# Hybrid streaming encoder on one core: the merge's first weights staged in the merge's own pool, the recurrence's state update in the PSUM bank of its outputs, four buffers for gate tiles

## The chip, the cores and the metric

The kernel runs on one core of one Trainium2 chip. Its time is the device time of one execution in microseconds (us); the time of a kernel is the median of its runs. The engines are named as in the profile: PE (TensorE, matmuls), PEld (its weight loads), DVE (VectorE), ACT (ScalarE), POOL (GpSimd) and SP (SyncE, which issues most DMAs). Every engine takes its instructions strictly in the order in which they stand in the program. SP does so too: a DMA that waits for a buffer holds up every DMA behind it.

## The reference, cut to what matters

One layer over 1024 prompt rows and 64 sample rows, model width 1024:

```
u = rms_norm(x)
proj = u @ w_in                      # four branches' inputs, and the gates
out_b = branch_b(proj)               # fox, diff, sb: attention; gdn: a recurrence
merged = sum_b sigmoid(gates_b) * (out_b @ w_branch[b])
x = x + merged @ w_out
x = x + swiglu(rms_norm(x))
y = rms_norm(x)

# gdn, per chunk of 64 rows:
v_new = u_i - kc_i @ S
o     = (q_i * exp(g_i)) @ S + a_i @ v_new
S     = S * exp(g_last) + (k_i * exp(g_last - g_i))^T @ v_new
```

The gates are a matmul of u with 4 x 1024 columns of `w_in`. They depend on nothing but u, so they can be computed at any time before the merge.

## The kernel before

The kernel is written as one long Python function; a scheduler then orders the instructions of each engine, by the priorities of the code and its own estimate of times. Precision is kept by splitting every operand into a high and a low float16 part, so that each product is three matmuls (`gemm_a`, lines 177 to 186).

The work goes in stages, and two of them matter here.

**The attention stages.** `attend_sb`, `attend_fox` and `attend_diff` run one after the other. In `attend_diff` (line 627) two pairs of heads go through nine tiles of 128 rows each, from the longest to the shortest. For one head of one tile PE computes scores (line 456, a mask at 458), DVE takes their maximum (646), ACT the exponential (655), DVE combines two softmaxes and splits the result, SP transposes it by DMA (`pt`, line 447), and PE multiplies by the values (lines 604 and 606). After each head `fill` (line 505) takes other work from two lists:

- `dense`: work that keeps PE busy. At this point it is `spill_gates` (line 1056). One call loads 256 columns of gate weights, in two DMAs of 512 KB to `w32` (line 149), splits them to `wh` (ACT) and `wl` (DVE), and computes six pieces of 128 gate rows, each of 24 matmuls to a bank `pgs`. ACT moves each piece to a tile `ths` in SBUF, and POOL's queue writes it to DRAM (line 1067).
- `side`: in `attend_diff` first the recurrence `gdn_seq` (line 896), one chunk of 64 rows per call, then `open_merge` (line 1128).

**The recurrence.** Each of 17 chunks computes `kc @ S` to `pks` (lines 1008 and 1009), `vn` on DVE, its split `vh`, the state update `pds` (12 matmuls, line 1021), the output `pog` (20 matmuls, lines 1024 to 1028), and the new state on DVE (line 1029), which is split to `Sh` and `Sl` for the next chunk. `prepare` (line 954) makes the next tile's operands. All PSUM tiles of the recurrence come from `pgd`, two banks: `pog` holds one for a whole tile, with `pks` in its upper half, and `pds`, `py`, `pu`, `pk` take turns.

**The merge.** `open_merge` closes the recurrence's pool and opens the merge's pool `br` in its place, then calls `load_branch` for `sb` and for `fox`. `load_branch` (line 1109) brings the branch's output (`oT`) and its two blocks of weights (512 KB each, line 1123), which are staged in `w32` and split to `wbh` and `wbl`, tiles of `br`. The loop from line 1162 then takes the branches in the order sb, fox, diff, gdn. For each of 24 pieces per branch it loads the gate tile from DRAM (`thg`), ACT applies tanh (1174), PE computes six matmuls to `ptb`, DVE multiplies, and DVE or POOL adds to the accumulators `mg`. For sb the gate tiles rotate over four buffers, for the others over twelve. `drain(dense)` (line 1140) puts whatever is left of the gates ahead of the merge's main part.

The staging tile `w32` has three buffers for the whole kernel. Each is held from the DMA's issue until DVE has made the low part from it:

```
w32 = wp.tile([P, 4, BW], F32, tag="w32", name="wb32", bufs=3)
wv = w32.rearrange("p a b -> p (a b)")[:, :D]
sync.dma_start(wv, i["w_branch"][0][j, k * P:(k + 1) * P])
acopy(wbh[:, k], wv, WS)
stt(wbl[:, k], wv, WS, wbh[:, k], ALU.mult, ALU.subtract)
```

Of the kernel before, what the change touches and what calls it, by code (L numbers as in the profile page):

```python
# [11 lines left out]
F32 = mybir.dt.float32  # L12
# [5 lines left out]
P = 128  # L18
D = 1024
KD = D // P  # L20
SEQ, SMP, PAST = 1024, 64, 256
T = SEQ + SMP
NT = 9
NH = 4
BW = 256
# [28 lines left out]
def tile_hybrid_encoder(ctx, tc, i, o):  # L54
# [8 lines left out]
    def stt(out, in0, s, in1, op0, op1):  # L63
        return vec.scalar_tensor_tensor(out=out, in0=in0, scalar=s, in1=in1, op0=op0, op1=op1)  # L64

    def tt(out, in0, in1, op, eng=None):
        return (eng or vec).tensor_tensor(out=out, in0=in0, in1=in1, op=op)
# [6 lines left out]
    def bc(ap, shape):  # L74
        return ap.to_broadcast(shape)
# [6 lines left out]
    wp = ctx.enter_context(tc.tile_pool(name="w", bufs=2, reuse_waits="tile"))  # L82
# [12 lines left out]
    def pgd(name="pgd"):  # L95
        return pp.tile([P, 512], F32, tag="g", name=name, bufs=2)
# [120 lines left out]
    sp = sp_.enter_context(tc.tile_pool(name="sp", bufs=1, side="right", reuse_waits="tile"))  # L217
# [674 lines left out]
    def new_state(S32, Sh, Sl):  # L892
        acopy(Sh, S32, 16.0)
        stt(Sl, S32, 16.0, Sh, ALU.mult, ALU.subtract)

    def gdn_seq(g3):
        ttbd = []
        for q in range(2):
            a = g3.tile([P, 2, NH, P], F16, name=f"ttbd{q}")
# [4 lines left out]
        for q in range(2):  # L904
            a = g3.tile([P, NH, 64], F32, name=f"tt32{q}")
# [6 lines left out]
        for q in range(2):  # L912
            a = g3.tile([P, 2, NH, 64], F16, name=f"vh{q}")
# [3 lines left out]
        def fresh_state():  # L917
            return (g3.tile([P, NH, 64], F16, tag="Sh", name="Sh", bufs=2),
                    g3.tile([P, NH, 64], F16, tag="Sl", name="Sl", bufs=2))
# [74 lines left out]
        for k, t in enumerate(order):  # L994
            after = load(order[k + 1]) if k + 1 < len(order) else None
            _, n, nch, u0, kc, kd, aa, qe, zt = here
            z4g = zt.rearrange("p (h e) -> p h e", h=NH)
            S32 = S32s if t == 8 else S32p
            if t in (8, 0):
                Sh, Sl = fresh_state()  # L1000
                new_state(S32, Sh, Sl)
            po = pgd("pog")
            pks = po[:, 256:512]
            for c in range(nch):
                sl = slice(64 * c, 64 * c + 64)
                e4 = eg[:, c, t * NH:(t + 1) * NH]
                for h in range(NH):
                    pe.matmul(pks[sl, h * 64:h * 64 + 64], lhsT=kc[:, h, sl], rhs=Sh[:, h], start=True, stop=False)
                    pe.matmul(pks[sl, h * 64:h * 64 + 64], lhsT=kc[:, h, sl], rhs=Sl[:, h], start=False, stop=True)
                S1 = g3.tile([P, NH, 64], F32, tag="S1", name="S1", bufs=2)  # L1010
                tt(S1, S32, bc(e4[:, :, None], [P, NH, 64]), ALU.mult)
                vn = g3.tile([P, NH, 64], F32, tag="vn", name="vn", bufs=2)
                vh = vhs[c]
                stt(vn[sl].rearrange("p h e -> p (h e)"), pks[sl, 0:256], -(2.0 ** -5),
                    u0[sl].rearrange("p h e -> p (h e)"), ALU.mult, ALU.add)
                acopy(vh[sl, 0], vn[sl])
                tt(vh[sl, 1], vn[sl], vh[sl, 0], ALU.subtract)
                pds = pgd("pds")
                for h in range(NH):
                    for q, (a, b) in enumerate(((0, 0), (0, 1), (1, 0))):  # L1020
                        pe.matmul(pds[:, h * 64:h * 64 + 64], lhsT=kd[:, a, h], rhs=vh[:, b, h], start=(q == 0), stop=(q == 2))
                for h in range(NH):
                    dst = po[sl, h * 64:h * 64 + 64]
                    pe.matmul(dst, lhsT=qe[:, h, sl], rhs=Sh[:, h], start=True, stop=False)
                    pe.matmul(dst, lhsT=qe[:, h, sl], rhs=Sl[:, h], start=False, stop=False)
                    pe.matmul(dst, lhsT=aa[:, 0, h], rhs=vh[:, 0, h], start=False, stop=False)
                    pe.matmul(dst, lhsT=aa[:, 0, h], rhs=vh[:, 1, h], start=False, stop=False)
                    pe.matmul(dst, lhsT=aa[:, 1, h], rhs=vh[:, 0, h], start=False, stop=True)
                stt(S32.rearrange("p h e -> p (h e)"), pds[:, 0:256], 2.0 ** -9, S1.rearrange("p h e -> p (h e)"), ALU.mult, ALU.add)
                Sh, Sl = fresh_state()  # L1030
                if not (t == 8 or (t == 7 and c == 1)):
                    new_state(S32, Sh, Sl)
                if c == 0 and after is not None:
                    here = prepare(*after)
                yield 0.0
            if t == 8:
                gps.dma_start(o["s_gdn_state"][0, 0].rearrange("h d e -> d h e"), S32[0:64])
            if t == 7:
                gps.dma_start(o["p_gdn_state"][0, 0].rearrange("h d e -> d h e"), S32[0:64])
            sq = g3.tile([P, NH, 64], F32, tag="sqo", name="sqo", bufs=1)  # L1040
            pov = po[:n, 0:256].rearrange("p (h e) -> p h e", h=NH)
            act.activation(sq[:n], pov, AF.Square)
            ss = g3.tile([P, NH], F32, tag="sso", name="sso", bufs=2)
            vec.tensor_reduce(out=ss[:n], in_=sq[:n], op=ALU.add, axis=AX.X)
            ts(ss[:n], ss[:n], 2.0 ** -18 / 64, EPS, ALU.mult, ALU.add, eng=gps)
            tt(ss[:n], ss[:n], mhb[:n, 0:NH], ALU.pow, eng=gps)
            tt(z4g[:n], z4g[:n], bc(ss[:n, :, None], [n, NH, 64]), ALU.mult)
            tt(z4g[:n], z4g[:n], pov, ALU.mult)
            os_ = g3.tile([P, 2, BW], F16, tag="osg", name="osg", bufs=2)
            acopy(os_[:n, 0], zt[:n])  # L1050
            tt(os_[:n, 1], zt[:n], os_[:n, 0], ALU.subtract)
            gps.dma_start(od["gdn"][t * P:t * P + n], os_[:n].rearrange("p l c -> p (l c)"))
# [3 lines left out]
    def spill_gates(b, sp, d2):  # L1056
        j = bidx[b]
        wu = load_unit([(w_in, 0, OFF_GATE + j * D + d2 * BW, BW)], BW)
        for m in range(2):
            d = 2 * d2 + m  # L1060
            for off, n in PIECES:
                pg = pd("pgs")
                gemm_a(pg, wu, m * P, uh, ul, off, n, KD)
                th = sp.tile([P, 364], F32, tag="ths", name="ths", bufs=2)
                with tc.high_priority():
                    acopy(th[:, :n], pg[:, :n], 0.5 * IWS)
                gps.dma_start(gtd[b][d * P:(d + 1) * P, off:off + n], th[:, :n])
                yield 3.7
# [40 lines left out]
    def load_branch(b):  # L1109

        brp, j = brps[0], bidx[b]
        oT = brp.tile([P, 2, 2, T], F16, tag="oT", name="oT", bufs=2)
        if b in ("sb", "fox"):
            for pr in range(2):
                gps.dma_start(oT[:, :, pr], od[b][pr])
        else:
            sync.dma_start_transpose(out=oT.rearrange("p l r t -> p (l r) t"), in_=od[b])
        wbh = brp.tile([P, 2, D], F16, tag="wbh", name="wbh", bufs=2)
        wbl = brp.tile([P, 2, D], F16, tag="wbl", name="wbl", bufs=2)
        for k in range(2):  # L1120
            w32 = wp.tile([P, 4, BW], F32, tag="w32", name="wb32", bufs=3)
            wv = w32.rearrange("p a b -> p (a b)")[:, :D]
            sync.dma_start(wv, i["w_branch"][0][j, k * P:(k + 1) * P])
            acopy(wbh[:, k], wv, WS)
            stt(wbl[:, k], wv, WS, wbh[:, k], ALU.mult, ALU.subtract)
        branch[b] = oT, wbh, wbl

    def open_merge():
        gd_.close()
        brps.append(br_.enter_context(tc.tile_pool(name="br", bufs=1, side="right", reuse_waits="tile")))  # L1130
        load_branch("sb")
        yield 0.0
        load_branch("fox")
        yield 0.0

    side += [gdn_seq(g3), open_merge()]
# [2 lines left out]
    brp = brps[0]  # L1139
# [16 lines left out]
    gt_pool = gp_.enter_context(tc.tile_pool(name="gates", bufs=1, reuse_waits="tile"))  # L1156

    pbk = (psc, pgd, psc, pgd, psc)
    nb_ = [0]
    mg = [(brp if d < 3 else gt_pool).tile([P, T], F32, tag=f"mg{d}", name=f"mg{d}") for d in range(KD)]  # L1160
    order = ("sb", "fox", "diff", "gdn")
    for bi, b in enumerate(order):
        if b not in branch:
# [5 lines left out]
        for d, (off, n) in [(d, PIECES[p]) for p in (0, 2, 1) for d in range(KD)] if last else \  # L1169
                [(d, p) for d in range(KD) for p in PIECES]:  # L1170
            th = (brp if bi == 0 else gt_pool).tile([P, 364], F32, tag=("th0" if bi == 0 else "th"), name="thg",
                                                    bufs=(4 if bi == 0 else 12))
# [366 lines left out]
```

## Time and profile before

| | |
|---|---|
| median of 3 runs | 1920.94 us (1919.0 to 1921.34) |
| the profiled execution's own time | 1923.47 us |
| its span, first to last instruction | 1921.5 us |
| PE busy | 92% of the span |
| DVE busy | 65% |
| ACT busy | 45% |
| POOL busy | 16% |
| granted TensorE clock, mean | 0.954 |

The table's shares are averages over the whole program. The kernel is bound by different things in different stages, so the stretches between about 640 and 1145 us are looked at one by one below. Times within the profile count from the span's start. A busy PE is an engine that has matmuls in flight; how fast they go depends on the granted clock.

### The profile page before, as it was taken

How to read it: one execution, taken by the hardware profiler on the slowest of the kernel's cores; microseconds unless marked ns; L12 is line 12 of the kernel's file. 1: busy time of each engine (PE TensorE's matmuls, PEld its weight loads, DVE VectorE, ACT ScalarE, POOL GpSimd, SP SyncE). 2: the span in 40 equal slices, each digit the busy share in tenths (PEclk: the TensorE clock that was granted, in tenths of full speed). 3: DMA queues.
4: the chain of work that ended last, by engine and by line, in shares of the span. 5: the costliest groups of instructions: out<-in, count | busy, mean ns of one | idle time of the engine just before them, and what ended most of it. 6: DMA issues, size and time to landing. Idle time of an engine off the chain costs nothing.

```text
span 1921.5 us, 36810 instructions
## 1 busy us (share of the span) xinstructions
PE 1767.0 (92%) x14364; PEld 1252.4 (65%) x14364; DVE 1249.0 (65%) x2589; ACT 868.2 (45%) x1819; POOL 310.3 (16%) x478
## 2 busy tenths in 40 slices
PE   7999898989977998766799889999999999999998
PEld 5678774656755565444466558886857758677573
DVE  7559773877776667889411997766646546556365
ACT  6335654998654455556522463433413314233142
POOL 2113341111001222212211661000000000000002
PEclk9999999999989999566899999999999999999999
DMA  6267789887989855444733955621211212112112
GB/s 222 44 108 218 224 234 215 168 179 155 208 191 210 183 148 128 94 108 84 262 107 103 280 153 144 121 83 34 78 44 45 67 32 79 45 45 67 33 45 99
DMA packets 412766, 244.28 MB, mean 127 GB/s; under 512 B 266278, under 2 KB 390450, under 8 KB 412456
## 3 DMA queue, kind: packets, MB, share of 16 engines
q1 hardware_dynamic: 398944, 205.67, 43.9%
q0 software_dynamic: 13648, 36.27, 6.5%
q8 instruction: 112, 1.84, 0.4%
q14 instruction: 62, 0.51, 0.1%
HBM read 123.39 MB, written 60.53 MB: 96 GB/s over the span
## 4 chain that ended last, share of the span: by engine, by line
PE 53%; DVE 8%; DMA 7%; issue 2%; ACT 1%; POOL 1%; SPq 0%; DVEq 0%; POOLq 0%; ACTq 0%
PE po L1461 12%; DMA pt<-st 4%; PE pgs L185 4%; PE pgs L183 3%; PE pgs L184 3%; PE pb L1345 3%; PE pb L1344 3%; PE pb L1346 3%; PE pc L1345 2%; PE pc L1346 2%; PE pa L1346 2%; PE pc L1344 2%; PE pa L1345 2%; PE pa L1344 2%; PE pout L165 1%
## 5 line engine op out<-in xcount | busy, mean ns | idle before, releaser
L183 PE MATMUL pgs<-u,wh 128*128 128x364 f16 (+1 forms) x768 | 245.1, 319 | 10.0 <-ACT ths L61 9.7
L184 PE MATMUL pgs<-u,wh 128*128 128x364 f16 (+1 forms) x768 | 245.2, 319 | 0.0
L185 PE MATMUL pgs<-u,wl 128*128 128x364 f16 (+1 forms) x768 | 244.7, 319 | 0.5 <-DVE wl L64 0.5
L1461 PE MATMUL po<-wh,hT 128*128 128x512 f16 (+1 forms) x792 | 238.1, 380 | 0.6 <-DVE x2a L64 0.6
L1461 PEld LDWEIGHTS <-hT 128*128 128x128 f16 (+1 forms) x1188 | 109.2, 99 | 120.0 <-issue 7.6
L64 DVE SCALAR_TENSOR_TENSOR x2a<-po,x2a 128x512 f32<-128x512 f32 x108 | 74.4, 689 | 141.6 <-PE po L1461 141.4
L61 ACT ACTIVATE wh<-w32f 128x1024 f16<-128x1024 f32 (+1 forms) x90 | 80.3, 926 | 160.6 <-PE po L1461 111.6
L1344 PE MATMUL pb<-X,wh 128*128 128x288 f16 (+1 forms) x528 | 147.1, 279 | 2.5 <-DMA X<-nsh 2.2
L1345 PE MATMUL pb<-X,wh 128*128 128x288 f16 (+1 forms) x528 | 147.2, 279 | 0.3 <-DMA X<-nsl 0.3
L1346 PE MATMUL pb<-X,wl 128*128 128x256 f16 (+1 forms) x528 | 146.3, 279 | 0.0
L64 DVE SCALAR_TENSOR_TENSOR wl<-w32f,wh 128x1024 f16<-128x1024 f32 (+1 forms) x90 | 94.6, 1065 | 79.2 <-ACT wh L61 79.1
L64 DVE SCALAR_TENSOR_TENSOR wl<-w,wh 128x1024 f16<-128x1024 f32 x62 | 74.8, 1229 | 108.8 <-ACT wh L61 80.3
L1461 PE MATMUL po<-wl,hT 128*128 128x512 f16 (+1 forms) x396 | 142.0, 379 | 0.0
L1344 PEld LDWEIGHTS <-wh 128*128 128x128 f16 x1232 | 120.5, 98 | 31.1 <-issue 2.3
L1345 PEld LDWEIGHTS <-wh 128*128 128x128 f16 x1232 | 120.5, 98 | 30.0 <-issue 2.4
L1346 PEld LDWEIGHTS <-wl 128*128 128x128 f16 x1232 | 120.5, 98 | 27.2 <-issue 0.9
L184 PEld LDWEIGHTS <-wh 128*128 128x128 f16 x912 | 89.6, 98 | 61.0 <-issue 11.8
L165 PE MATMUL pd<-wh,u 128*128 128x256 f16 (+1 forms) x448 | 123.8, 276 | 1.5 <-ACT e L61 1.5
L167 PE MATMUL pd<-wh,u 128*128 128x256 f16 (+1 forms) x448 | 123.5, 276 | 0.0
L166 PE MATMUL pd<-wl,u 128*128 128x256 f16 (+1 forms) x448 | 123.5, 276 | 0.0
L183 PEld LDWEIGHTS <-wh 128*128 128x128 f16 x912 | 89.7, 98 | 51.7 <-issue 1.7
L185 PEld LDWEIGHTS <-wl 128*128 128x128 f16 x912 | 89.6, 98 | 51.4 <-issue 1.2
(393 smaller groups left out, 4647.4 us busy)
## 6 DMA issues: line engine op xcount, KB each, us to landing
w<-in_w_in_dram SPq DMA_DIRECT2D x56, 512.0 KB, 5.3
w32f<-in_w_ffn_gate_dram SPq DMA_DIRECT2D x20, 512.0 KB, 4.9
w32f<-in_w_ffn_up_dram SPq DMA_DIRECT2D x20, 512.0 KB, 3.9
w32f<-in_w_ffn_down_dram SPq DMA_DIRECT2D x20, 512.0 KB, 4.1
xt<-in_x_prompt_dram SPq DMA_DIRECT2D x8, 512.0 KB, 6.8
wb<-in_w_branch_dram SPq DMA_DIRECT2D x8, 512.0 KB, 4.9
w<-in_w_out_dram SPq DMA_DIRECT2D x8, 512.0 KB, 4.9
x2a<-in_x_prompt_dram SPq DMA_DIRECT2D x8, 512.0 KB, 8.4
```

What stands on the lines that cost most here:

```text
L61: return act.activation(out, in_, AF.Copy, scale=scale)
L64: return vec.scalar_tensor_tensor(out=out, in0=in0, scalar=s, in1=in1, op0=op0, op1=op1)
L165: pe.matmul(ps[:n, :N], lhsT=a, rhs=wh[:, k, :N], start=(k == 0), stop=False)
L166: pe.matmul(ps[:n, :N], lhsT=a, rhs=wl[:, k, :N], start=False, stop=False)
L167: pe.matmul(ps[:n, :N], lhsT=b, rhs=wh[:, k, :N], start=False, stop=(k == K - 1))
L183: pe.matmul(ps[:, :n], lhsT=a, rhs=xh[:, k, off:off + n], start=(k == 0), stop=False)
L184: pe.matmul(ps[:, :n], lhsT=a, rhs=xl[:, k, off:off + n], start=False, stop=False)
L185: mm = pe.matmul(ps[:, :n], lhsT=b, rhs=xh[:, k, off:off + n], start=False, stop=(k == K - 1))
L1344: pe.matmul(ps[:, :n], lhsT=wh[:, k], rhs=xh_, start=(start and k == 0), stop=False, skip_group_check=not start)
L1345: pe.matmul(ps[:, :n], lhsT=wh[:, k], rhs=xl_, start=False, stop=False, skip_group_check=not start)
L1346: mm = pe.matmul(ps[:, :n], lhsT=wl[:, k], rhs=xh_, start=False, stop=(k == 3), skip_group_check=not start)
L1461: pe.matmul(ps[h * n:h * n + n], lhsT=hts[k + h][:, a, tk:tk + n], rhs=w[:, k + h], start=(k == 0 and a == 0 and w is wh), stop=(k + nh >= ...
```

## The change

Three edits. The weights of the branch sb, the first that the merge needs, are staged in the memory of the accumulators `mg0` and `mg1` (tiles of `br` that are not written before), instead of in `w32`; the call for fox goes out of `open_merge`, so that the merge's loop makes it; and to make room `mg2` moves from `br` to the pool of the gate tiles. The recurrence's `pds` is the upper half of `pog`'s bank, where `pks` lies. The gate tiles `ths` get four buffers instead of two.

```
@@ gdn_seq
             po = pgd("pog")
-            pks = po[:, 256:512]
+            pks = pds = po[:, 256:512]
...
-                pds = pgd("pds")
@@ spill_gates
-                th = sp.tile([P, 364], F32, tag="ths", name="ths", bufs=2)
+                th = sp.tile([P, 364], F32, tag="ths", name="ths", bufs=4)
@@ load_branch
         for k in range(2):
-            w32 = wp.tile([P, 4, BW], F32, tag="w32", name="wb32", bufs=3)
-            wv = w32.rearrange("p a b -> p (a b)")[:, :D]
+            if b == "sb":
+                wv = brp.tile([P, T], F32, tag=f"mg{k}", name="wb32")[:, :D]
+            else:
+                w32 = wp.tile([P, 4, BW], F32, tag="w32", name="wb32", bufs=3)
+                wv = w32.rearrange("p a b -> p (a b)")[:, :D]
@@ open_merge
         load_branch("sb")
-        yield 0.0
-        load_branch("fox")
         yield 0.0
@@ merge
-    mg = [(brp if d < 3 else gt_pool).tile([P, T], F32, tag=f"mg{d}", name=f"mg{d}") for d in range(KD)]
+    mg = [(brp if d < 2 else gt_pool).tile([P, T], F32, tag=f"mg{d}", name=f"mg{d}") for d in range(KD)]
```

The edits move instructions, since the scheduler orders them anew. Up to the first chunk of the recurrence every engine's order is as before; from the first out-projection on it is the same again. Between the two it differs. Three places follow; lines 1018 to 1119 of the kernel before are one lower in the changed kernel, and line 1123 is line 1125.

SP, early in the diff stage, after the second transpose of the second tile (`tt`, `t`, `rec1b`, `qe`: operands of the recurrence; `pt`, `qt`: of the attention; `wb`: branch weights; `w`: gate weights). Before:

```order
L943 DMA rec1b<-r1d 128x1536
L447 DMA_TRANSPOSE pt<-st 128x14x128
L1123 DMA wb_11963<-in_w_branch_dram 128x1024
L1123 DMA wb_12085<-in_w_branch_dram 128x1024
L447 DMA_TRANSPOSE pt<-st 128x12x128
L491 DMA_TRANSPOSE qt<-qd_diff 128x4x128
L937 DMA tt_8738<-xd 32x4x32
```

The same place in the changed kernel:

```order
L447 DMA_TRANSPOSE pt<-st 128x14x128
L940 DMA t_9911<-xtd 32x4x32
L937 DMA tt_8738<-xd 32x4x32
L938 DMA tt_8738<-xd 32x4x32
L939 DMA tt_8738<-nd 32x4x32
L940 DMA t_9911<-xtd 32x4x32
L149 DMA w_12169<-in_w_in_dram 128x4x256
L149 DMA w_12589<-in_w_in_dram 128x4x256
```

Three loads of branch weights (sb's two and fox's first; one stands some rows further up) are gone from here, and loads of gate weights stand in their place. Before, no load of gate weights follows until after the last `pt` of the stage, where ten come; now all ten stand within the stage, seven of them behind these two.

SP, near the end of the diff stage in the changed kernel (`w_..<-in_w_out` are weights of the out-projection, `thg` gate tiles for the merge, `wb_11942` and `wb_11946` the weights of sb):

```order
L149 DMA w_14096<-in_w_out_dram 128x4x256
L447 DMA_TRANSPOSE pt<-st 128x8x128 x2
L491 DMA_TRANSPOSE qt<-qd_diff 128x4x128
L447 DMA_TRANSPOSE pt<-st 128x6x128
L1125 DMA wb_11942<-in_w_branch_dram 128x1024
L1125 DMA wb_11946<-in_w_branch_dram 128x1024
L1173 DMA thg<-gtd_sb 128x364 x2
L1173 DMA thg<-gtd_sb 128x360
L447 DMA_TRANSPOSE pt<-st 128x6x128
```

The weights of sb now stand ahead of the last seven transposes of the diff stage, and the weights of fox (not shown) some twenty rows higher, behind the last load of gate weights.

PE, at the scores of one tile of the second pair of heads, counted from the stage's end in both. Before:

```order
L604 MATMUL po<-vt,pt 128x128
L606 LDWEIGHTS pt
L606 MATMUL po<-vt,pt 128x64
L456 LDWEIGHTS qt
L456 MATMUL psc<-kT,qt 128x512
L458 LDWEIGHTS identb
L458 MATMUL psc<-mk_diff,identb 128x128
L456 LDWEIGHTS qt
L456 MATMUL psc<-kT,qt 128x512
L1024 LDWEIGHTS qe
```

In the changed kernel:

```order
L1009 MATMUL pog<-Sl,kc 64x64
L962 MATMUL py<-t_10649,tt_8738 32x32 x4
L456 LDWEIGHTS qt
L456 MATMUL psc<-kT,qt 128x512
L183 LDWEIGHTS wh
L183 MATMUL pgs<-u_103,wh 128x364
L184 LDWEIGHTS wh
L184 MATMUL pgs<-u_103,wh 128x364
L185 LDWEIGHTS wl
L185 MATMUL pgs<-u_103,wl 128x364
```

Gate matmuls (`pgs`) now stand between the attention's own all through the stage, where before there are none in its last three fifths. The twelve `pds` matmuls of a chunk are followed at once by its twenty `pog` matmuls, and the new state on DVE waits for the last of the twenty, where it waited for the last of the twelve before.

## Rows read from the trace of the kernel before

**Rows 1.** Windows: busy time of each engine in five stretches.

```profile
core 0: us, PE busy (x) PEld busy (x) DVE busy (x) ACT busy (x) POOL busy (x), PEclk, DMA share, GB/s
640.00:760.00 120.00, 118.23 (x1104) 76.28 (x1101) 81.24 (x237) 60.01 (x155) 29.96 (x50) 1.00 0.63 147
760.00:919.00 159.00, 102.55 (x1107) 74.62 (x1107) 139.51 (x510) 88.59 (x272) 40.09 (x66) 0.60 0.45 99
919.00:937.00 18.00, 11.39 (x58) 6.42 (x58) 8.07 (x12) 10.26 (x15) 4.32 (x7) 0.69 0.87 308
937.00:1055.60 118.60, 118.13 (x769) 75.00 (x768) 20.57 (x25) 35.03 (x66) 15.76 (x29) 1.00 0.42 142
1055.60:1144.30 88.70, 76.70 (x475) 46.49 (x474) 79.42 (x122) 48.14 (x92) 55.85 (x51) 0.98 0.77 225
```

**Rows 2.** Windows of the gate pieces' instructions (tile pgs) alone, three of these stretches.

```profile
640.00:760.00 120.00, 92.60 (x552) 11.27 (x24) 1.00 0.63 147
760.00:919.00 159.00, 0.00 (x0) 0.00 (x0) 0.60 0.45 99
937.00:1055.60 118.60, 111.41 (x718) 13.51 (x29) 1.00 0.42 142
```

**Rows 3.** Timeline of SP: start us, us; a load of gate weights, then branch weights.

```profile
670.19 1.26 SPq L149 DMA_DIRECT2D w<-in_w_in_dram  x1
...
672.11 0.40 SPq L1123 DMA_DIRECT2D wb<-in_w_branch_dram  x1
...
696.69 2.40 SPq L1123 DMA_DIRECT2D wb<-in_w_branch_dram  x2
```

**Rows 4.** Timeline of ACT: the first instructions that read those branch weights.

```profile
919.53 2.93 ACT L61 ACTIVATE wbh<-wb 128x1024 f16<-128x1024 f32 x3
```

**Rows 5.** Chain that ended last, between 919 and 937: start us, us, what.

```profile
925.54 9.84 DMA w<-in_w_in_dram
```

**Rows 6.** Tile wl, 640 to 1060: ns min/median/max, first and last start us.

```profile
L64 DVE SCALAR_TENSOR_TENSOR wl<-w,wh x20: 1215/1222/1226, 638.9 to 1058.3; 128x1024 f16<-128x1024 f32 x20
```

**Rows 7.** Waits of PE, 640 to 760 (the only one): us, times, longest us.

```profile
PE po L604 <- DMA pt<-st: 0.6, 1, 0.6
```

**Rows 8.** Waits of PE, 760 to 920, the longest in total.

```profile
PE po L604 <- DMA pt<-st: 15.7, 11, 3.6
PE psc L456 <- ACT p L655: 10.9, 18, 1.8
```

**Rows 9.** Timeline of ACT at the first gate pieces, early in the sb stage.

```profile
300.82 0.47 ACT L61 ACTIVATE ths<-pgs 128x360 f32<-128x360 f32 x1 [12.21 <-DMA gtd_sb<-ths]
```

**Rows 10.** Timeline of SP there: loads of the attention's first q.

```profile
304.45 7.50 SPq L491 DMA_TRANSPOSE qt<-qd_sb  x3
```

**Rows 11.** Tile qt there, the same three loads, from issue to landing.

```profile
DMA to landing us min/median/max: 5.2/5.8/8.7
```

**Rows 12.** Timeline of PE there: the first scores, for which it did not wait.

```profile
314.27 0.38 PE L456 MATMUL psc<-kT,qt 128*128 128x512 f16 x1
```

**Rows 13.** Tile thg, 937 to 1060: tanh, sb's products, gate tiles from issue to landing.

```profile
L1174 ACT ACTIVATE thg<-thg x26: 487/502/507, 939.6 to 1059.2; 128x364 f32<-128x364 f32 x17, 128x360 f32<-128x360 f32 x9
...
L64 DVE SCALAR_TENSOR_TENSOR mg<-thg,ptb x17: 521/530/534, 943.7 to 1059.9; 128x364 f32<-128x364 f32 x11, 128x360 f32<-128x360 f32 x6
...
DMA to landing us min/median/max: 2.3/4.6/5.9
```

**Rows 14.** Tile ptb, 900 to 1150: the products of fox, diff and gdn.

```profile
L64 DVE SCALAR_TENSOR_TENSOR thg<-thg,ptb x72: 514/519/533, 1064.1 to 1149.0; 128x364 f32<-128x364 f32 x48, 128x360 f32<-128x360 f32 x24
```

**Rows 15.** Timeline of DVE: new states of two chunks that follow each other.

```profile
908.53 0.41 DVE L64 SCALAR_TENSOR_TENSOR S32p<-pds,S 128x256 f32<-128x256 f32 x1
...
913.87 0.42 DVE L64 SCALAR_TENSOR_TENSOR S32p<-pds,S 128x256 f32<-128x256 f32 x1 [0.26 <-PE pds L1021]
```

**Rows 16.** Timeline of PE: outputs of the second chunk, first and last of 17.

```profile
913.76 0.26 PE L1027 MATMUL pog<-vh,rec2b 128*64 128x64 f16 x1
...
914.64 0.24 PE L1028 MATMUL pog<-vh,rec2b 128*64 128x64 f16 x1
```

## The prediction

> **What bounds the kernel now.** I read the windows first, since shares of the whole span mix stages. From 640 to 760 PE is busy 118.2 of 120 us at the full clock (1.00 is the level of 2.4 GHz), DVE 81 us: PE is the bound [rows 1]. From 760 to 919 it is DVE, busy 139.5 of 159 us; PE is busy 102.6 us, but at a mean clock of 0.60, that is mostly at 1.2 GHz [rows 1]. From 937 to 1055.6 PE works without a gap and DVE is nearly idle (20.6 us) [rows 1]. The windows of the gate pieces alone say why: 552 gate matmuls in the first stretch, none in the second, 718 in the third [rows 2]. The gates are the filling of the attention stage. It ran out at 760, the stage went on at DVE's pace, and the filling was worked off afterwards with nothing beside it.
>
> It did not run out for want of gates, but for want of staging buffers. SP issued a load of gate weights at 670.2, and then three loads of branch weights at 672.1, 696.7 and right after it [rows 3]. Each holds one of the three `w32` buffers until it is converted to `wbh` and `wbl`. Those are tiles of the merge's pool, which lies where the recurrence's pool lies, and the first conversion ran at 919.5 [rows 4], after the recurrence. So from about 700 all three buffers were full of data that nobody could use, and the next gate weights were loaded at 925.5, when the chain of waits stands on that load for 9.8 us [rows 5].
>
> **The change part by part.**
>
> *Branch weights.* sb's two loads now go to the merge's own memory and touch no `w32`. fox's two still do, but the new order puts them behind the last gate load, so the five units of gate weights (ten loads) that came after 919 come inside the diff stage.
>
> What PE then has to do from 760 on: a gate matmul takes 118.6 / 769 = 0.154 us where PE does only such [rows 1]. In the first stretch 552 of 1104 matmuls are gates (85.0 us), so the other 552 took the remaining 33.2 us, 0.060 us each at the full clock [rows 1, 2]. The second stretch's 1107 others cost 1107 x 0.060 = 66.4 us at that rate; the gates left are 722 (718 and four before 937), 722 x 0.154 = 111.2 us. Sum 177.6 us: the gates end at 760 + 177.6 = 937.6 instead of 1055.6, and with PE full I expect the clock to stay at its upper level, as it did from 640 to 760.
>
> DVE must fit beside that: 139.5 us, and ten low parts of gate weights at 1.22 us [rows 6], 151.7 us, or 85% of 177.6. ACT has 89 us and as many conversions. Both fit, DVE with little room.
>
> *The merge.* What is late next is sb's part of it, which lay beside the lonely gates before. Its gate tiles rotate over four buffers: 4.6 us from issue to landing, 0.50 tanh, 0.53 product [rows 13], and 0.34 for the issue is a round of about 6.0 us for four pieces, 1.5 us a piece, where PE needs 6 x 0.154 = 0.92. 24 pieces take 36 us from 937.6: to 973.6. The last heads of the diff stage lie beside them. From there I take the old pace: 1064.1, the first product of fox, to the end of the merge's matmuls at 1144.3 is 80.2 us [rows 1, 14]. The merge ends at 1053.8, 90.5 us earlier. Best case: sb at the whole merge's pace, 88.7 us for some 471 of its 576 matmuls [rows 1], ends at 937.6 + 108.5 = 1046, 8 us better.
>
> sb's weights now stand in SP's queue ahead of the last seven `pt` transposes, and must wait for the recurrence's pool. Released 4.7 us after the recurrence's last matmul (914.9 to 919.5) [rows 4, 16] and loaded in at most 9.8 us, as a load of the same size was [rows 5], they could hold up PE for 14.5 us. The cover: in the new order about 100 gate matmuls (15.4 us) stand between the last outputs and the first merge matmul. I take 0, and 14.5 as the upper bound. The fox weights and the move of `mg2` cost 0: the first are loaded while gates run, the second is written late.
>
> *State update in the bank of the outputs.* It frees a bank for `prepare`, and makes the new state wait for all outputs. 17 outputs follow each other in 0.9 us [rows 16], so 20 take 1.1 us, and 17 chunks 19 us of the recurrence's chain. I take 0, since the chain has room (17 chunks of 5.3 us [rows 15] are 91 us in a stage three times as long) and PE did not wait for it while it had gates: from 640 to 760 it waited 0.6 us in all, from 760 to 920 some 15.7 us for `pt` alone [rows 7, 8]. The bounds are 0 and 19. The Trainium skill has a rule against this edit: its page "PSUM — Partial Sum Buffer", section "PSUM bank collisions raise a hardware error", tells to read a bank other than the one that TensorE writes, and to guard by bank. Before, DVE read `pds` from 913.9 while PE wrote `pog` [rows 15, 16], in two banks, so the trace shows no such collision; by the rule the wait is unavoidable, and if it lay on the path the sum would be some 19 us worse.
>
> *Four gate tiles.* ACT waited 12.2 us for a spill, before the first scores of the sb stage [rows 9]. But the scores need q, issued at 304.45 and landing 8.7 us later at most, at 313.2, and they ran at 314.3 [rows 10, 11, 12]. Worth 1.1 us; from below the bound is a few us lost (the spills go out earlier, onto the same DMA engines as q).
>
> **Sum.** 90.5 + 1.1 = 91.6 us. The profiled execution took 1923.47 us, 2.5 above the median of 1920.94; against the median this gives 1829.3, about 1829 us.
>
> **The rivals.**
>
> *The two streams don't fit beside each other.* DVE sets the pace at 88% busy (139.5 of 159), so its 151.7 us need 172 us, against PE's 177.6: both are at their limit, and each will wait for the other. If that costs 15%, the stage ends 27 us later: 1856. For it speaks DVE's share; against it that from 640 to 760 PE was 98.5% busy beside DVE at 68%. Chance 0.22.
>
> *Slower: the recurrence paces PE.* PE takes matmuls in order. If at each of 17 chunks it stood idle for the whole chain, 5.3 us [rows 15] and 1.1 for the shared bank, it would lose 17 x 6.4 = 109 us, more than is won: 1829 + 109 = 1938. It decides from 91.6 / 17 = 5.4 us lost a chunk on. Against it speaks the wait of 0.6 us with gates in the queue [rows 7]. Chance 0.03. The Trainium skill's page "PSUM — Partial Sum Buffer" (the section above) bears on this rival: its rule is what lengthens the chain.
>
> *The buffers stay blocked.* If fox's two loads catch two of three buffers before the gates are through, nothing moves: about 1921. The new order has them behind the last gate load. Chance 0.02.
>
> **How the numbers follow.** The forecast keeps 0.73. Its own bounds: 8 us better for sb's pace and some 5% of 177.6 us for PE's mean; worse by 14.5 for SP's wait and part of the 19. The range goes from 1808 to 1866, which takes in the first rival with 10 us to spare. A measurement of this kernel tells 0.2%, about 4 us, from no change. Faster by more: the forecast and the first rival, 0.95; same 0.02; slower 0.03.
>
> **What would show it.** Right: no branch weights loaded before 880, gate matmuls throughout the diff stage, the clock at its upper level from 760 to 930, no stretch with gates alone, and a merge of 105 to 120 us after the last gate. The first rival shows as PE busy under 90% with waits for DVE and `pt`. The prediction is wrong if gates still pile up after the last `pt`, if PE waits over 5 us a chunk for `Sh`, `Sl` or `vn`, or if the merge takes more than 140 us.

## The result and the profile after

The changed kernel takes 1833.93 us (median of 4 runs, 1830.35 to 1847.62), the kernel before 1921.14 beside it: ratio 0.9555, 95% interval 0.95 to 0.9609. The forecast was 1829, the range 1808 to 1866.

The profiled execution of the changed kernel is its slowest, 1847.62 us, with a span of 1845.9. It lost 10 us before the recurrence's first chunk, where the two programs are still the same: that chunk starts at 670.7 us, in the kernel before at 660.7. So stages are compared from that chunk on. Windows of the changed kernel: busy time of each engine from 650 to the end of the merge.

```profile
core 0: us, PE busy (x) PEld busy (x) DVE busy (x) ACT busy (x) POOL busy (x), PEclk, DMA share, GB/s
650.00:770.00 120.00, 116.38 (x1183) 78.13 (x1181) 86.75 (x253) 62.89 (x162) 27.33 (x48) 0.99 0.72 163
770.00:943.00 173.00, 169.39 (x1694) 114.36 (x1695) 138.68 (x433) 100.44 (x266) 52.73 (x85) 0.99 0.64 153
943.00:968.00 25.00, 16.28 (x114) 9.99 (x113) 19.01 (x75) 17.95 (x54) 5.56 (x11) 0.86 0.87 260
968.00:1069.00 101.00, 84.44 (x511) 50.87 (x511) 83.11 (x138) 57.89 (x116) 57.06 (x55) 0.95 0.78 228
```

The gate pieces alone, the same view:

```profile
650.00:770.00 120.00, 86.51 (x510) 9.84 (x21) 0.99 0.72 163
770.00:943.00 173.00, 128.08 (x754) 14.47 (x31) 0.99 0.64 153
943.00:1069.00 126.00, 0.00 (x0) 0.45 (x1) 0.93 0.80 234
```

Against [rows 1, 2]: in the stretch that held no gate matmul there are now 754, PE is busy 98% of it, and the clock is at its upper level (0.99, where it was 0.60). The lonely gates are gone. The last gate matmul starts at 942.66, the first of the merge at 942.82. What PE waited for from 670 to 943, and then from 943 to 1075 (the two longest):

```profile
PE po L604 <- DMA pt<-st: 5.7, 4, 1.9
PE psc L456 <- ACT p L655: 0.8, 1, 0.8
PE py L962 <- DMA tt<-nd: 0.7, 1, 0.7
...
PE ptb L183 <- DVE thg L64: 10.6, 10, 2.7
PE ptb L183 <- DVE mg L64: 7.8, 5, 4.4
```

PE does not wait for the recurrence, and loses little to DVE before 943 [rows 7, 8]. From there on it waits for DVE: the merge's last matmul starts 126 us after the last gate, where the prediction had 116.

Of one kernel below, state_in_scores_bank, the profile fell on an execution of 4580 us, so the table has nothing but its median, 1902.93 us without that execution and 1906.25 with it.

### The profile page after: what moved, and what is told of

Read it like the earlier page. It is cut to its first block, busy times and chain, and to the rows that moved or that the text cites. A ratio compares the mean times of both kernels' runs of the same rounds, so it can differ in the third digit from the quotient of the medians.

```text
span 1845.9 us, 36819 instructions
## 1 busy us (share of the span) xinstructions
PE 1731.1 (94%) x14364; PEld 1228.5 (67%) x14364; DVE 1248.7 (68%) x2589; ACT 866.2 (47%) x1819; POOL 305.9 (17%) x478
## 4 chain that ended last, share of the span: by engine, by line
PE 53%; DMA 8%; DVE 6%; issue 2%; ACT 2%; POOL 1%; SPq 0%; DVEq 0%; POOLq 0%; ACTq 0%
PE po L1461 12%; DMA pt<-st 3%; PE pb L1345 3%; PE pb L1344 3%; PE pb L1346 3%; PE pgs L185 3%; PE pgs L184 3%; PE pgs L183 3%; PE pc L1345 2%; PE pa L1344 2%; PE pa L1346 2%; PE pa L1345 2%; PE pc L1346 2%; PE pc L1344 2%; PE pout L165 1%
## 5 line engine op out<-in xcount | busy, mean ns | idle before, releaser
L183 PEld LDWEIGHTS <-wh 128*128 128x128 f16 x912 | 90.1, 99 | 51.1 <-issue 1.4
```

Of the source, the lines that this page charges most:

```text
L183: pe.matmul(ps[:, :n], lhsT=a, rhs=xh[:, k, off:off + n], start=(k == 0), stop=False)
```

## The experiments

All were timed beside the kernel before on their chip; its own median there lay between 1921.14 and 1928.89 us. In the table, times in the last six columns are us after the first `pks` matmul of the recurrence in the profiled execution, read off PE's timeline; the column "chunk 1" is that matmul's own start. Up to it PE's order is the same in all of them, but for the last eight matmuls in state_in_po_bank, and in u_in_gates_bank, where it stands 133 matmuls earlier.

| kernel | median, us | ratio (95%) | chunk 1 | recurrence ends | gates end | diff ends | merge starts | merge ends |
|---|---|---|---|---|---|---|---|---|
| before | 1921.14 | | 660.7 | 254 | 395 | 254 | 265 | 483 |
| changed | 1833.93 | 0.956 (0.950, 0.961) | 670.7 | 253 | 272 | 297 | 272 | 398 |
| again | 1832.67 | 0.953 (0.948, 0.957) | 655.5 | 249 | 267 | 293 | 267 | 395 |
| staging_and_bank | 1831.71 | 0.951 (0.946, 0.956) | 663.5 | 250 | 269 | 294 | 269 | 395 |
| staging_only | 1867.37 | 0.970 (0.966, 0.974) | 668.0 | 297 | 258 | 288 | 310 | 418 |
| bank_only | 1900.45 | 0.987 (0.982, 0.992) | 660.2 | 216 | 365 | 318 | 235 | 461 |
| fox_out_only | 1862.81 | 0.967 (0.964, 0.970) | 653.8 | 289 | 261 | 279 | 301 | 418 |
| fox_out_and_bank | 1841.57 | 0.957 (0.954, 0.961) | 670.9 | 250 | 266 | 299 | 272 | 398 |
| third_sum_early | 1844.69 | 0.958 (0.955, 0.961) | 670.0 | 248 | 267 | 295 | 268 | 395 |
| seven_gate_tiles | 1831.03 | 0.953 (0.949, 0.956) | 658.7 | 249 | 268 | 294 | 268 | 393 |
| state_in_po_bank | 1865.2 | 0.970 (0.966, 0.974) | 660.9 | 248 | 263 | 325 | 278 | 429 |
| state_in_scores_bank | 1902.93 | 0.988 (0.984, 0.992) | | | | | | |
| u_in_gates_bank | 1906.18 | 0.992 (0.989, 0.994) | 655.4 | 220 | 363 | 361 | 245 | 471 |
| later_recurrence | 1883.0 | 0.976 (0.970, 0.983) | 673.0 | 314 | 250 | 284 | 326 | 434 |

### The parts of the change, one by one

**again**: the changed kernel, unaltered.

> The changed kernel once more, as the measure for the three that follow. Expected 1834 us, between 1828 and 1845: the gates end about 272 us after the recurrence's first chunk, the merge 126 us after the gates. If the first 10 us that the profiled execution of the changed kernel lost before 670 us (13.8 us of idle PE for q at the start of the sb stage) belong to the change, they are there again; if they were one execution's accident, the first chunk starts near 661 us.

1832.67 us, and the first chunk at 655.5: the 10 us were that execution's own. Of the 15.2 us between the two profiles 8.8 lie at the start of the sb stage, where PE waits for `qt`: 13.78 us in the first profile, 4.98 in this one. Most of the rest are PE's waits for `pt` in the stages between, 26.3 us against 19.0. First the changed kernel, then this run, PE's timeline:

```profile
319.01 0.61 PE L456 MATMUL psc<-kT,qt 128*128 128x512 f16 x1 [13.78 <-DMA qt<-qd_sb]
```

```profile
311.73 0.61 PE L456 MATMUL psc<-kT,qt 128*128 128x512 f16 x1 [4.98 <-DMA qt<-qd_sb]
```

Over all profiles the first chunk starts between 653.8 and 673.0, and the executions of the kernel before, timed beside these runs, go from 1909.78 to 1937.32 us. So single kernels' medians that are 10 us apart need the columns behind it.

**staging_and_bank**:

```
-                th = sp.tile([P, 364], F32, tag="ths", name="ths", bufs=4)
+                th = sp.tile([P, 364], F32, tag="ths", name="ths", bufs=2)
```

> The change with two buffers for the gate tiles ths instead of four: every engine's instructions stand as in the changed kernel. Theory (the four buffers are worth 1 us): within 4 us of the changed kernel, 1830 to 1838, and the idle time before the first scores of the sb stage is some 9 us in two parts, as in the kernel before. Rival (four buffers send the spills out earlier and delay q on the same DMA engines): 4 to 10 us faster than the changed kernel, 1824 to 1830. Rival (the buffers free ACT and so PE): 5 to 10 us slower.

1831.71 against 1832.67 us, and every column behind chunk 1 within 2 us: the four buffers bring nothing that can be measured. (Before the first scores PE is idle for 9.2 and 2.0 us here, where some 9 us were expected.)

**staging_only** is that, and the second edit undone:

```
-            pks = pds = po[:, 256:512]
+            pks = po[:, 256:512]
...
+                pds = pgd("pds")
```

> Only the first edit: sb's weights staged in mg0 and mg1, fox's load out of the opening, mg2 moved; the state update in its own bank, two ths. Theory (the staging carries everything, the shared bank nothing): 1828 to 1845, gates beside the whole diff stage and the clock at its upper level there. Rival (the shared bank is what lets the recurrence run beside the gates, since it frees a bank for the next tile's operands): 1860 to 1921, with PE waiting for py, pu or pk. Rival (the shared bank costs one microsecond a chunk on the path): 1815 to 1828.

1867.37 us: 36 us slower than with the bank, within the first rival's range, though with another wait than it named. The windows after the last gate show the loss:

```profile
926.00:965.00 39.00, 24.98 (x294) 19.48 (x292) 33.10 (x131) 22.64 (x71) 12.04 (x21) 0.60 0.51 147
965.00:978.00 13.00, 0.20 (x4) 0.17 (x3) 5.52 (x8) 9.43 (x18) 5.30 (x8) 0.50 0.58 193
978.00:1086.00 108.00, 94.41 (x574) 57.22 (x574) 82.93 (x137) 55.34 (x109) 51.42 (x49) 0.97 0.75 228
```

The gates end even earlier (258 against 269), but the recurrence ends 39 us after them. The merge's pool lies in its memory, so no merge matmul can start before: for 52 us PE has the rest of the diff stage and the recurrence alone, mostly at the lower clock level. Why the recurrence is late stands in PE's timeline, at one change of tile. Staging alone:

```profile
751.62 0.22 PE L1008 MATMUL pog<-Sh,kc 128*64 128x64 f16 x1
...
758.17 0.43 PE L962 MATMUL py<-t,tt 32*32 32x32 f32 x8
...
762.60 0.43 PE L965 MATMUL py<-tt,y 32*32 32x32 f32 x8
767.58 0.22 PE L980 MATMUL pu<-rec1b,ttbd 128*128 128x64 f16 x2
...
769.77 0.78 PE L983 MATMUL pk<-ttbd,rec1b 128*128 128x128 f16 x11
773.12 0.51 PE L1021 MATMUL pds<-vh,rec2b 128*128 128x64 f16 x12
```

The same place in **again** (`pds` is now written as `pog`, line 1020):

```profile
721.99 0.22 PE L1008 MATMUL pog<-Sh,kc 128*64 128x64 f16 x1
...
726.12 0.22 PE L980 MATMUL pu<-rec1b,ttbd 128*128 128x64 f16 x2
...
727.55 0.19 PE L1020 MATMUL pog<-vh,rec2b 128*128 128x64 f16 x1
...
728.66 0.48 PE L1020 MATMUL pog<-vh,rec2b 128*128 128x64 f16 x11
...
731.54 0.83 PE L983 MATMUL pk<-ttbd,rec1b 128*128 128x128 f16 x12
```

A tile's second chunk begins with the first row. In its own bank its state update (`pds`) comes 773.12 - 751.62 = 21.5 us later, behind the next tile's `py`, `pu` and `pk`, which take both banks in turn; in the shared bank its first matmul comes 5.6 us later and the other eleven 6.7, ahead of `pk`. PE does not stand still meanwhile, it has gates to do; but the next state, and with it the next tile, waits for the update. From a tile's second chunk to the next tile's first it takes 24 us on average of seven with staging alone (14 to 29), and 15 in **again** (12 to 21). That is the wait which the prediction did not see: a turn of two banks among five tiles.

By the merge's end the bank is worth 418 - 395 = 23 us here, by the medians 36. The two profiled executions differ by 1864.04 - 1838.66 = 25.4 us, of which 4.5 lie before chunk 1; the other 10 us of the 36 are how far each of the two lay from its kernel's median.

**bank_only**: the second edit alone.

> Only the second edit: the state update in the bank of the outputs, the weights staged as before. Theory (the gates stay blocked, the chain of the recurrence has room): 1917 to 1925, as the kernel before. Rival (the shared bank lengthens a chain that paces PE where it has no gates): up to 17 x 1.1 = 19 us slower, 1925 to 1940, with PE waits for Sh or vh between 760 and 919 us. Rival (the freed bank speeds the recurrence): 1900 to 1917.

1900.45 us, 28 better than the 1928.89 of the kernel before beside it: the second rival. SP's timeline shows how:

```profile
699.17 2.39 SPq L1122 DMA_DIRECT2D wb<-in_w_branch_dram  x2
892.20 0.44 SPq L1122 DMA_DIRECT2D wb<-in_w_branch_dram  x1
893.07 1.51 SPq L149 DMA_DIRECT2D w<-in_w_in_dram  x2
```

The staging buffers are as blocked as before [rows 3], but the recurrence ends at 216 instead of 254, so gate weights flow again at 893 instead of 925 [rows 5], beside the last 85 us of the diff stage. Measured by the merge's end, staging brings 65 us, the bank 23, both 88: the parts add up. By the medians they are 62, 28 and 97.

### Is it the freed bank?

Three kernels put a tile of the recurrence into other banks: `pds` into the scores' three (`psc`), `pds` into the single `po` bank (both with staging alone), and `pu` into the gate pieces' two (with staging and the shared bank):

```
-                pds = pgd("pds")
+                pds = psc("pds")     # state_in_scores_bank
+                pds = pso("pds")     # state_in_po_bank
-            pu = pgd("pu")
+            pu = pd("pu")            # u_in_gates_bank
```

> The first edit, with the state update pds neither in its own turn of the recurrence's two banks nor in that of the outputs, but in the three banks of the attention's scores. Theory (what the second edit brings is the freed bank: with the staging alone the state update of a tile's second chunk waited for a bank behind the next tile's py, pu and pk, and the change of tile took some 25 us instead of 16): the recurrence ends some 40 us earlier than with the staging alone, before the gates, and the time is 1825 to 1845. Rival (it is the sharing itself, or the order that the scheduler happens to find with it): 1860 to 1875, as with the staging alone. Rival (a bank taken from the scores costs what the freed one brings): about 1850.

> The first edit, with the state update pds in the single bank of the diff stage's own outputs (po): the recurrence's two banks are freed of it as by the second edit, but it shares no bank with pog, and the gates stand spread over the diff stage nearly as in the changed kernel (the last of them before the 201st of 208 scores). Theory (the freed bank is the gain): 1828 to 1845, the recurrence done before the gates, a tile in about 28 us instead of 37; the po of the attention may wait some us for pds. Rival (the sharing itself is the gain): 1860 to 1875. Rival (any other bank loses what it brings, as the scores' bank seemed to): 1850 to 1900.

> Staging and bank, with pu of the recurrence in the banks of the gate pieces, so that pk need not wait for pog. The recurrence ends sooner by some 25 of the 208 scores, and the gates last to the end of the diff stage (5 pieces left at the last scores, where the changed kernel has none from the 201st on). Theory (gates under the stage's last scores cover its tail): 5 to 15 us faster than staging and bank, 1817 to 1827. Rival (the gates are then thinner in the middle of the stage, and DVE sets the pace there): the same or slower, 1832 to 1850.

All three miss the theory's time. The second, 1865.2 us, lies in the range of both its rivals, so its time decides nothing. Of the recurrence the second shows what the theory said: it ends at 248, as with the shared bank, without sharing. So freeing the bank makes it early, with the order that the scheduler makes of it, and sharing is not needed. But the gain is lost behind it. From 918 on, after the recurrence's end, the merge's loads start, and they meet `pt` transposes. Windows of this kernel, and then of **again** at the same point:

```profile
918.00:925.00 7.00, 6.45 (x61) 4.35 (x60) 5.92 (x19) 3.23 (x10) 4.27 (x7) 1.00 0.97 264
925.00:938.00 13.00, 0.49 (x12) 0.43 (x9) 6.82 (x13) 8.22 (x13) 1.39 (x3) 0.69 1.19 102
```

```profile
914.00:921.00 7.00, 7.00 (x53) 4.48 (x52) 5.66 (x23) 4.33 (x10) 4.31 (x7) 1.00 1.08 320
921.00:934.00 13.00, 7.50 (x56) 4.83 (x55) 10.71 (x35) 11.40 (x30) 2.01 (x4) 0.88 1.06 322
```

The DMA engines are full in both (a share of 1.19 and of 1.06), but move 102 GB/s in the one and 322 in the other. The chain of waits of state_in_po_bank has one `pt` there, and its four `oT` loads of 544 KB land late (7.2 to 11.8 us in **again**):

```profile
921.54 20.67 DMA pt<-st
```

```profile
DMA to landing us min/median/max: 16.6/18.3/19.4
```

The diff stage ends 31 us later than in **again**. PE's waits there, 918 to 990, show where part of it goes:

```profile
PE ptb L183 <- DMA oT<-od_sb: 13.4, 1, 13.4
PE po L604 <- DVE o L64: 11.9, 10, 3.1
```

The first is the late `oT`; of the second **again** has 3.0 us from 914 to 955. That the rest follows from the same jam is argued, not shown.

In the other two the scheduler put the gates elsewhere. The 208 scores counted here are those of the sb and the diff stage together, and the last 104 are the diff stage's. With `pds` among the scores, the last gate stands in PE's order right behind the 161st (the 201st in the changed kernel), so the last 47 scores of the stage have no filling; that this is the loss was not measured by itself. With `pu` among the gates, 42 pieces of 24 gate matmuls are left at the 144th, where the changed kernel has 31: the gates end at 363, and from 760 to 850 PE is busy 71 of 90 us at a clock of 0.77.

```profile
760.00:850.00 90.00, 71.00 (x754) 47.89 (x753) 75.30 (x255) 47.12 (x138) 23.49 (x39) 0.77 0.53 122
```

**later_recurrence** goes the other way, with staging alone:

```
-                if c == 0 and after is not None:
+                if c == nch - 1 and after is not None:
                     here = prepare(*after)
```

> Staging alone, with the next tile's operands prepared after a tile's last chunk instead of its first: nothing is computed otherwise, but the recurrence is longer, and five of its 17 chunks stand behind the last scores of the diff stage instead of two. Theory (what the shared bank brought was an earlier end of the recurrence, on which the merge's pool and so sb's part wait): three chunks more in the lonely tail, some 12 us each: 20 to 40 us slower than staging alone, 1887 to 1907, the gates ending as before about 258 us after the first chunk and the first merge matmul 330 us or more after it (310 with staging alone, 267 with both). Rival (the bank acts in another way, and the recurrence's end is hidden): within 5 us of 1867.

1883.0 us, 15.6 slower than staging alone. The size is below what was expected, but the relation is close: the recurrence ends 16.6 us later, the merge starts 15.9 and ends 15.9 later, though the gates end 9 us earlier.

### The pieces of the staging edit, and the merge

**fox_out_only** leaves sb's weights in `w32` and `mg2` in `br`, and takes only the call out; **fox_out_and_bank** adds the shared bank:

```
         load_branch("sb")
         yield 0.0
-        load_branch("fox")
-        yield 0.0
```

> Only fox's load is taken out of the opening; sb's two weights are staged in the common buffers as before, bank and ths as before. Theory (sb's two hold two of the three staging buffers until the recurrence ends, so gate weights go through one buffer, but do go): gates in the whole diff stage, somewhat thinner than with the staging alone; with the late recurrence of that kernel, 1862 to 1885. Rival (one buffer left is as good as none, since a unit of gate weights takes two): 1900 to 1930. Rival (sb's staging in its own pool is not needed): 1862 to 1870.

> Fox's load out of the opening and the shared bank; sb's weights in the common staging buffers, mg2 where it was, two ths. Theory (sb's staging in the merge's pool is worth nothing, since one free buffer carries the gate weights: with the recurrence late, 1863 against 1867): 1826 to 1840, the changed kernel's time with two of its five pieces. Rival (with a recurrence that is early, the buffers that sb's two weights hold delay the gates, or the merge, by 10 us or more): 1842 to 1860.

1862.81 us: what the first edit brings, it brings by fox's load. SP's timeline of fox_out_only: sb's weights hold two of the three buffers from 689.72 on, and the gate weights pass one by one through the third.

```profile
689.72 0.36 SPq L1123 DMA_DIRECT2D wb<-in_w_branch_dram  x1
691.78 0.38 SPq L149 DMA_DIRECT2D w<-in_w_in_dram  x1
722.98 0.38 SPq L149 DMA_DIRECT2D w<-in_w_in_dram  x1
729.70 0.39 SPq L149 DMA_DIRECT2D w<-in_w_in_dram  x1
```

The gates end at 261, where 258 was with staging alone. There the merge starts 9.5 us earlier than with staging alone and still ends at 418, so an earlier start is not always an earlier end. With the bank, 1841.57 us, between the theory's range and the rival's, and a merge that ends at 398, against 395. By that, sb's staging in the merge's pool is worth some 3 us. The medians are 10 us apart; in the profiles 7.4 us lie before the first chunk, and whether the edit has a part in that is not shown.

**third_sum_early** and **seven_gate_tiles**, both on staging_and_bank:

```
-    mg = [(brp if d < 2 else gt_pool).tile(...
+    mg = [(brp if d < 3 else gt_pool).tile(...     # third_sum_early
...
-                                                    bufs=(4 if bi == 0 else 12))
+                                                    bufs=(7 if bi == 0 else 12))     # seven_gate_tiles
```

> Staging and bank, with mg2 back in the merge's own pool (two ths, so that it has room). Theory (with mg2 in the gate tiles' pool, which opens only after the diff stage, sb's seventh to ninth product wait; PE stands for 4 us once): three pieces more run beside the diff stage, 2 to 5 us faster than staging and bank, 1826 to 1830. Rival (the pace of the diff stage's tail, or the gate tiles' loads, set the end): within 2 us of it, 1830 to 1834.

> Staging and bank, with seven buffers instead of four for sb's gate tiles in the merge (two ths, so that there is room). Theory (sb's 24 pieces go at the round of four buffers, 1.5 us a piece against PE's 0.92): up to 10 us faster than staging and bank, 1822 to 1828. Rival (they wait for the sums mg3 and on, whose pool opens after the diff stage, so more buffers only wait there): within 3 us of it, 1829 to 1835.

The second's 1831.03 us lies in its rival's range, the first's 1844.69 in neither. Neither moves the merge's end by more than 2.4 us (395 and 393 against 395). The median of the first, 13 us worse, is not explained by that: in its profile 6.5 us of it lie before the first chunk, where no engine's order differs, and the cause of that and of the rest is open. sb's products on DVE, in the changed kernel:

```profile
961.03 0.52 DVE L64 SCALAR_TENSOR_TENSOR mg<-thg,ptb 128x364 f32<-128x364 f32 x1
961.74 0.52 DVE L64 SCALAR_TENSOR_TENSOR mg<-thg,ptb 128x360 f32<-128x360 f32 x1
972.07 1.85 DVE L64 SCALAR_TENSOR_TENSOR mg<-thg,ptb 128x364 f32<-128x364 f32 x4
```

Six products, those of `mg0` and `mg1`, run before the gap, and with `mg2` in `br` exactly nine. The others wait for the pool of the gate tiles, which opens after the diff stage (its last output matmul is at 968.06). From there to the merge's end it takes 99 to 102 us in all six kernels in which the recurrence and the gates end before the diff stage and the loads are undisturbed. That points to the end of the diff stage as what sets the merge's end. A merge without that wait was not tried.

No version is measurably faster than the changed kernel.

## Why the prediction was right, and where it was not

- **The gates beside the diff stage: right.** Predicted 276.9 us after the first chunk (937.6 - 660.7), measured 272.0 and 267.2. The clock and DVE (138.68 of 173 us busy) did as said, no stretch has gates alone, and the first rival, that the streams don't fit, fell: PE waited 7.2 us in 273. One sign of being right failed without harm: branch weights were to come after 880, and fox's first load came earlier, behind the last load of gate weights as the order had it. SP's timeline of the changed kernel:

```profile
850.43 0.33 SPq L1125 DMA_DIRECT2D wb<-in_w_branch_dram  x1
```

- **The shared bank: the step that failed.** "I take 0, since the chain has room", with bounds 0 and +19. It brought 36 us beside the staging and 28 alone (23 in both cases by the merge's end). The row taken for a chunk [rows 15] was the last tile's, the only one with no next tile to prepare, so 5.3 us had no turn of banks in it. The chunks' mean there is 249.3 / 16 = 15.6 us, so the chain fills nearly all of the stage, and not a third of it: its last matmul, at 914.6, stands at the stage's end. The cost that was seen is small. DVE's waits for the state update, in all, times and longest, first in **again** from 655 to 905 and then in staging_only, with `pds` in its own bank, from 668 to 966:

```profile
DVE S32p L64 <- PE pog L1027: 5.1, 7, 1.5
DVE S32p L64 <- PE pds L1021: 4.2, 3, 2.1
```

Taken from each chunk's last `pds` matmul to the new state's start on DVE, it is 16.2 us over the 17 chunks in **again** and 7.3 in staging_only: some 9 us, where the upper bound was 19.

The Trainium skill's page "PSUM — Partial Sum Buffer", section "PSUM bank collisions raise a hardware error", asks to guard by bank; that guard is the wait for the outputs, and the traces price it at these few us, while the bank that was freed was worth more.

- **The staging: right in its end, wrong in its share.** The prediction took the recurrence's end from before and let the staging bring 90.5 us. With gates beside it the recurrence of the kernel before ends at 297, not 254, and staging brings 65 us. The bank took those 43 us back, so that the two errors cancelled: 253 after, 254 before. That the sum came out within 5 us is luck in this part. Both parts stand in the table: 483 to 418 and 418 to 395.
- **sb's weights behind the recurrence: 0, right** for the changed kernel, whose first merge matmul starts 0.16 us after the last gate's, but narrowly. The recurrence's last matmul starts at 924.0, and the weights are issued 10.6 us behind it, where 4.7 were taken; DVE makes the second low part just before that first matmul at 942.82. SP's timeline, then DVE's:

```profile
934.61 1.11 SPq L1125 DMA_DIRECT2D wb<-in_w_branch_dram  x2
...
941.26 1.21 DVE L64 SCALAR_TENSOR_TENSOR wbl<-wb,wbh 128x1024 f16<-128x1024 f32 x1
```

The gates that were left covered it. Near the upper bound of 14.5 came staging_only, with its late recurrence: 13 us without a matmul, 965 to 978 in its windows.
- **sb's part of the merge: mis-sized.** 36 us were taken, for four buffers, from the last gate to the first product of fox; that product starts 993.8 - 942.7 = 51.1 us after it, and sb's own last 55.7. That products wait for the sums' pool is a delay that the prediction did not have; how much of the 15 us it makes was not measured. The four gate buffers hold sb's last product back too: with seven it starts 45.1 us after the last gate, but the merge's end does not move with it. `mg2`'s move cost nothing that the merge's end shows. The rest went faster than the old pace: from 993.8 to the end of the last matmul at 1069.4 it is 75.6 us instead of 80.2. So the merge took 126 us after the last gate, outside the 105 to 120 named as a sign of being right.
- **Four gate tiles: 1.1 taken, nothing measured.** q's own loads vary by more.

Sum: 91.6 us predicted, 1921.14 - 1833.93 = 87.2 measured, and in **again** 1928.89 - 1832.67 = 96.2.

## What to carry to other kernels

When two parts of a change meet in one resource, price each with the other in place: the recurrence's end looked fixed because the filling that would delay it had run out. A chain's step is to be read at a place where everything that shares its buffers is running, and a bank that is given up may cost a short wait and remove a long one. What releases a memory pool is worth a row of its own: with staging alone the merge could not start before the recurrence's end, and when that came 16.6 us later the merge ended 15.9 later. Once the recurrence ends before the gates, that no longer holds.

## What was not expected of the hardware

- Transposes beside bulk loads jammed once: in the profile of state_in_po_bank the DMA engines were busy throughout for 13 us and moved 102 GB/s, where the same loads, with other transposes around them, ran at 322 in **again**. What decides between the two is open.
- The first chunk starts at 670.7 and 655.5 us in two profiles of the same program. Over kernels with the same order of PE up to it, it starts up to 19 us apart (653.8 in fox_out_only, 673.0 in later_recurrence), and 18.4 of that is there at the first scores of the sb stage (310.2 and 328.6).
